# Turning more activations by transposing transfers, issued from ScalarE's queue, in a two-layer encoder trunk

## The chip, the cores and the metric

The kernel runs on one core of a Trainium2 chip. The metric is the device time of one execution in microseconds; the median of several executions is compared. TensorE does the matrix products and the transpositions by identity, ScalarE (ACT) and VectorE (DVE) the elementwise work, GpSimd (POOL) a little, and SyncE (SP) issues most transfers.

## The reference

256 tokens of width 1024 pass two layers. Each layer has one wide projection, two parallel branches, a merge, a feed-forward part and an embedding term. All is float32.

```python
u = rms_norm(h, g_mix_pre)
(gq, gk, gv, gg, ra_f, ra_b, aq, ak, av, gate_a, gate_b) = jnp.split(u @ w_in, offsets, axis=-1)
# branch A: gated linear attention in both directions, 4 heads
o_gla = rms_norm(o_f + o_b, g_gla_out).reshape(b, s, GLA_VAL)
branch_a = (o_gla * jax.nn.silu(gg)) @ w_o_gla
# branch B: grouped-query attention, 8 query heads in 2 groups, axial rotary positions
q = apply_axial_rope(rms_norm(aq.reshape(b, s, ATTN_HEADS, HEAD_DIM), g_q_norm), cos, sin)
branch_b = gqa_attention(q, k, v) @ w_o_attn
mixed = jax.nn.sigmoid(gate_a) * branch_a + jax.nn.sigmoid(gate_b) * branch_b
h = h + rms_norm(mixed @ w_out, g_mix_post)
gate, up = jnp.split(rms_norm(h, g_ffn_pre) @ w_ffn_in, 2, axis=-1)
h = h + rms_norm((jax.nn.silu(gate) * up) @ w_ffn_out, g_ffn_post)
h = h + rms_norm(jax.nn.sigmoid(h @ w_ple_gate) * (p_i @ w_ple_proj), g_ple_post)
```

## The kernel before, in words

Every float32 operand x of a product is split into a high part (x rounded to the type fp32r) and a low part (x minus the high part), and a product is three passes: high by high, high by low, low by high. `split` (L134) makes both parts: ScalarE casts, VectorE subtracts. A weight unit is 1 MB: SP loads it into one of two raw buffers, ScalarE and VectorE split it into one of four pairs of buffers wh and wl (two pieces each), and TensorE uses it in 24 matmuls (`amode` and `passes`, L122, for both halves of 128 tokens). `Stream` keeps the order of the units: `done` frees a pair, starts the next load and places the next splits. Some gates and feed-forward blocks are computed in seven products instead of eight (`seven`, 12 matmuls each); VectorE makes the sums of weights for these (L326 to L337), in tiles called "lent" and "big".

An activation that is the left operand of a product must lie with its channels on the partitions, so it has to be turned. `transpose_in` (L449) does that on TensorE for a block of four 128x128 tiles: four transpositions by the identity into a PSUM bank "aux", then `split` from PSUM. This serves the normalised inputs, the gated output of branch A (tiles "gg" turned into a `Split` object gT), the mix (mixT), the attention's queries (L1267, four heads a group and half) and others.

In the feed-forward part the hidden activations are turned by transfers already, save those of the last pair of blocks. `turn_out` copies the block on ScalarE so that the upper and lower 16-bit words stand apart (L463 or L468), and a transposing transfer of 2-byte elements (L469), issued by SP, turns them. Some ticks later `take_in` joins the words by another copy on ScalarE (L476) and splits the result from SBUF.

The order of the work is fixed when the program is built. Each engine runs its instructions in the order that a planner gives it, mostly that of the program; `high_priority` puts a group of instructions ahead by that many places. Small tasks are generators: `tick` is called after every six matmuls of width 512, and a task yields the number of ticks after which it wants to go on. `need` runs a task to its end at once, for the user of a result. In the gate stage the order is the string GATES: u is a unit of the first branch's gate, a digit one of the seven products of the second's, m a unit of branch A's output projection, which needs gT. Then come the merge (attention's output projection) and "wout", the product of the mix with w_out, first for the first half of the tokens and then for the second.

Of the kernel before, what the change touches and what calls it, by code (L numbers as in the profile page):

```python
# [27 lines left out]
WAIT, WAIT_FIRST = 6, 4  # L28

WAIT_NEXT, WAIT_IN, WAIT_H = (7, 9), ((6, 9), (6, 6)), ((3, 5), (3, 5))  # L30
WAIT_MIX = 3, 6
WAIT_SPREAD = 12
W = dict(r=5, z=6, s0=4, s=3, s1=9, o0=1, o=1, k=4, q=3, a0=1, a1=4, a2=4, a3=1, g=6)

STEPS_FIRST = "00 10 01 11 02 12 03 13".split()
STEPS = "00 01 02 10 03 11 12 13".split()
# [24 lines left out]
def trunk_kernel(ctx: ExitStack, tc: tile.TileContext, a: dict, out: bass.AP):  # L61
# [390 lines left out]
        if plain is not None:  # L452
            nc.scalar.copy(plain, ps[:, : n * P])

    def turn_out(src, k, hf):

        with tc.high_priority(AHEAD):
            both, turned = halves(mid())
            turned = turned.bitcast(U16)
            parts = both.bitcast(U16).rearrange("p (s c) -> p s c", s=2)  # L460
            words = src.bitcast(U16)
            if hf is None:
                nc.scalar.copy(  # L463
                    parts.rearrange("p s (k h f) -> p s k h f", k=2, f=P),
                    words.rearrange("p (h k f s) -> p s k h f", h=2, f=P, s=2),
                )
            else:
                nc.scalar.copy(parts, words.rearrange("p (c s) -> p s c", s=2))  # L468
            nc.sync.dma_start_transpose(out=turned.rearrange("p (x t) -> p x t", t=P), in_=parts.rearrange("p s c -> p (s c)"))  # L469
        return both, turned  # L470

    def take_in(sp, both, turned, k, hf):

        n, tn = (2, T) if hf is None else (4, P)
        hi, lo = sp.at(k, n, (hf or 0) * P, tn)
        nc.scalar.copy(  # L476
            both.bitcast(U16).rearrange("p (k t s) -> p k t s", s=2, t=tn),
            turned.rearrange("p (s k t) -> p k t s", s=2, t=tn),
        )
        split(hi, lo, both.rearrange("p (k t) -> p k t", t=tn))  # L480

    last_pow = [None]

# [565 lines left out]
    for l in range(DEPTH):  # L1049
# [210 lines left out]
        def attend(g):  # L1260
            qs = []
            for hf in range(2):
                yield W["q"]
                ps = aux()
                for i in range(4):
                    hd = 4 * g + i
                    nc.tensor.transpose(ps[:, i * P : (i + 1) * P], qrs[hf][:, hd * P : (hd + 1) * P], ident)  # L1267
                qh, ql = halves(mid(F32R))
                split(qh, ql, ps)
# [193 lines left out]

        ogate = Task(out_gate(), f"{l}gg")

# [49 lines left out]
        def merge(br):  # L1515
            def then(j, hf, o):
                sl = [s[:, hf, j * 512 : (j + 1) * 512] for s in sgate[: br + 1]]
                vmul(sl[br], o, sl[br])
                if br == 1:
                    nc.vector.tensor_tensor(out=sl[0], in0=sl[0], in1=sl[1], op=ALU.add)  # L1520
# [46 lines left out]


        part[0] = f"{l}ffnin"
        hid = Split()  # L1570
        us = [[ws.take() for _ in range(2)] for _ in range(2)]

        def turned(src, k, hf):

            def turn():
                if k == 2 * PAIRS[-1]:
                    yield WAIT_LAST[hf]
                    transpose_in(hid, src, k, 4, hf)
                else:
                    x = turn_out(src, k, hf)  # L1580
                    yield WAIT_TURNED
                    take_in(hid, *x, k, hf)
# [193 lines left out]
```

## Time and profile before

| | us |
|---|---|
| median of 3 runs | 908.38 (907.43 to 909.86) |
| the profiled execution | 909.68 |
| its span | 907.9 |
| TensorE busy | 898.8 |
| VectorE busy | 790.2 |
| ScalarE busy | 620.5 |
| GpSimd busy | 105.9 |

Engines in the rows are PE (matmul), PEld (weight load, beside PE), DVE, ACT, POOL and SP; a q behind the name is the engine's queue of instructions. L134 is line 134 of the kernel. Instructions that issue transfers are not counted as busy. A row of the groups gives the line, the engine, the operation, the tile written and the tiles read, shapes and count, then busy time and mean ns, then idle time just before with what ended it. In a timeline a row begins with its start and its length. The 0 or 1 in a tile's name is the layer, and the letters behind it the part of the program.

### The profile page before, as it was taken

The page shows a single profiled execution, that of the slowest core. Times are in us where ns is not written, and L with a number is a line of the kernel's source. Part 1 is how long each engine was busy: PE and PEld are TensorE (multiplying, and loading weights), DVE is VectorE, ACT ScalarE, POOL GpSimd, SP SyncE. Part 2 cuts the span into 40 slices and gives each one's busy share as a digit, 9 for nine tenths or more (in the row PEclk, how much of TensorE's full clock was granted, in tenths as well). Part 3 has the DMA queues.
Part 4 walks back from the last instruction along what each step waited for, and adds up shares of the span by engine and source line. Part 5 has one row for each costly group of instructions (what it writes and reads, how often), then busy time and mean ns, then how long its engine had stood idle before and what let it go on. Part 6 is the DMA issues. An engine that isn't in the chain of part 4 may idle for free.

```text
span 907.9 us, 12157 instructions
## 1 busy us (share of the span) xinstructions
PE 898.8 (99%) x4479; PEld 762.2 (84%) x4479; DVE 790.2 (87%) x1021; ACT 620.5 (68%) x1011; POOL 105.9 (12%) x157
## 2 busy tenths in 40 slices
PE   9999999999999999999999999999999999999997
PEld 8898888888888887887898888888888888888886
DVE  7999989987668999998779899799876799999984
ACT  7688677564467787756676687675644796958563
POOL 3700221300100000000254001110000000000001
PEclk9999999999999999999999999999999999999999
DMA  8663445657397594956576424455573966858461
GB/s 283 219 189 136 140 140 191 216 187 249 115 288 204 173 301 146 317 170 233 180 279 204 168 93 140 139 186 185 186 241 100 309 180 206 254 210 264 150 231 47
DMA packets 108519, 178.16 MB, mean 196 GB/s; under 512 B 22494, under 2 KB 46566, under 8 KB 107948
## 3 DMA queue, kind: packets, MB, share of 16 engines
q1 hardware_dynamic: 108300, 177.25, 59.9%
q8 instruction: 35, 0.57, 0.3%
q14 instruction: 24, 0.20, 0.1%
q10 hardware_dynamic: 160, 0.14, 0.0%
HBM read 169.50 MB, written 3.15 MB: 190 GB/s over the span
## 4 chain that ended last, share of the span: by engine, by line
PE 78%; DVE 11%; DMA 4%; issue 4%; ACT 2%; POOL 0%; SPq 0%; POOLq 0%; ACTq 0%; DVEq 0%
PE acc_1ffnin L122 12%; PE acc_0gate L122 7%; PE acc_1gate L122 7%; PE acc_1ffnin L106 7%; DVE wl_0ffnin L134 6%; PE acc_1rq L122 3%; PE acc_0gqk L106 2%; PE acc_1gqk L106 2%; PE acc_1wout L122 2%; PE acc_0ple L122 2%; PE acc_1v L122 2%; PE acc_0gg L122 2%; PE acc_1gg L122 2%; PE acc_0v L122 2%; PE acc_0merge L122 2%
## 5 line engine op out<-in xcount | busy, mean ns | idle before, releaser
L134 ACT CAST wh_0ffnin<-raw_0ffnin 128x1024 fp32r<-128x1024 f32 x38 | 38.1, 1048 | 19.8 <-DMA raw_0ffnin<-in_w_ffn_out_dram 10.2
L134 ACT CAST wh_1ffnin<-raw_1ffnin 128x1024 fp32r<-128x1024 f32 x38 | 38.3, 1048 | 17.4 <-DMA raw_1ffnin<-in_w_ffn_out_dram 5.0
L134 DVE TENSOR_TENSOR wl_0ffnin<-raw_0ffnin,wh_0ffnin 128x1024 fp32r<-128x1024 f32 x38 | 44.6, 1219 | 5.8 <-ACT wh_0ffnin L134 5.8
L134 DVE TENSOR_TENSOR wl_1ffnin<-raw_1ffnin,wh_1ffnin 128x1024 fp32r<-128x1024 f32 x38 | 44.8, 1219 | 5.0 <-ACT wh_1ffnin L134 4.9
L106 PE MATMUL acc_0ffnin<-wh_0ffnin,big_0ffnin 128*128 128x512 f32 x176 | 45.4, 392 | 0.0
L106 PE MATMUL acc_1ffnin<-wh_1ffnin,big_1ffnin 128*128 128x512 f32 x176 | 45.1, 390 | 0.0
L122 PE MATMUL acc_0ffnin<-wh_0ffnin,big_0wout 128*128 128x512 f32 x168 | 41.8, 390 | 0.0
L122 PE MATMUL acc_1ffnin<-wh_1ffnin,big_1wout 128*128 128x512 f32 x168 | 41.5, 389 | 0.0
L106 PEld LDWEIGHTS acc_0ffnin<-wh_0ffnin,big_0ffnin 128*128 128x128 f32 x176 | 32.8, 188 | 7.5 <-DVE big_0ffnin L134 0.5
L106 PEld LDWEIGHTS acc_1ffnin<-wh_1ffnin,big_1ffnin 128*128 128x128 f32 x176 | 33.0, 188 | 6.9
L122 PEld LDWEIGHTS acc_0ffnin<-wh_0ffnin,big_0wout 128*128 128x128 f32 x168 | 31.4, 188 | 7.1 <-ACT wh_0ffnin L134 0.4
L122 PEld LDWEIGHTS acc_1ffnin<-wh_1ffnin,big_1wout 128*128 128x128 f32 x168 | 31.5, 188 | 6.5
L134 DVE TENSOR_TENSOR wl_1ffnin<-lent_1ffnin,wh_1ffnin 128x1024 fp32r<-128x1024 f32 x30 | 35.7, 1217 | 0.6 <-ACT wh_1ffnin L134 0.6
L134 DVE TENSOR_TENSOR wl_0ffnin<-lent_0ffnin,wh_0ffnin 128x1024 fp32r<-128x1024 f32 x30 | 35.6, 1216 | 0.1
L134 ACT CAST wh_1ffnin<-lent_1ffnin 128x1024 fp32r<-128x1024 f32 x30 | 30.7, 1051 | 5.4 <-PE acc_1ffnin L106 3.9
L134 ACT CAST wh_0ffnin<-lent_0ffnin 128x1024 fp32r<-128x1024 f32 x30 | 30.4, 1053 | 3.6 <-DVE lent_0ffnin L332 3.4
L134 ACT CAST wh_0gate<-raw_0gate 128x1024 fp32r<-128x1024 f32 x20 | 19.9, 1049 | 14.4 <-DMA raw_0gate<-in_w_o_attn_dram 6.1
L134 ACT CAST wh_1gate<-raw_1gate 128x1024 fp32r<-128x1024 f32 x20 | 19.9, 1048 | 13.9 <-PE acc_1gate L122 5.9
L134 DVE TENSOR_TENSOR wl_0gate<-raw_0gate,wh_0gate 128x1024 fp32r<-128x1024 f32 x20 | 24.2, 1257 | 5.2 <-ACT wh_0gate L134 5.1
L134 DVE TENSOR_TENSOR wl_1gate<-raw_1gate,wh_1gate 128x1024 fp32r<-128x1024 f32 x20 | 23.5, 1221 | 5.1 <-ACT wh_1gate L134 5.1
L106 PE MATMUL acc_0ffnin<-wl_0ffnin,big_0ffnin 128*128 128x512 f32 x88 | 24.6, 394 | 0.6 <-DVE wl_0ffnin L134 0.6
L106 PE MATMUL acc_1ffnin<-wl_1ffnin,big_1ffnin 128*128 128x512 f32 x88 | 24.0, 391 | 0.0
(730 smaller groups left out, 2731.7 us busy)
## 6 DMA issues: line engine op xcount, KB each, us to landing
raw_0ffnin<-in_w_ffn_out_dram SPq DMA_DIRECT2D x11, 1024.0 KB, 5.9
raw_1ffnin<-in_w_ffn_out_dram SPq DMA_DIRECT2D x11, 1024.0 KB, 5.5
lent_0ffnin<-in_w_ffn_in_dram SPq DMA_DIRECT2D x6, 1024.0 KB
lent_1ffnin<-in_w_ffn_in_dram SPq DMA_DIRECT2D x6, 1024.0 KB, 7.5
raw_0v<-in_w_in_dram SPq DMA_DIRECT2D x4, 1024.0 KB, 5.8
raw_0gate<-in_w_o_gla_dram SPq DMA_DIRECT2D x4, 1024.0 KB, 6.8
raw_0gate<-in_w_o_attn_dram SPq DMA_DIRECT2D x4, 1024.0 KB, 5.2
raw_0wout<-in_w_ffn_in_dram SPq DMA_DIRECT2D x8, 512.0 KB, 4.6
```

What stands on the lines that cost most here:

```text
L106: return nc.tensor.matmul(o, lhsT, rhs, start=start, stop=stop)
L122: nc.tensor.matmul(o, x, y, start=start and n == 0, stop=stop and n == len(seq) - 1, **kw)
L134: return nc.scalar.copy(hi, src), nc.vector.tensor_tensor(out=lo, in0=src, in1=hi.bitcast(F32), op=ALU.subtract)
```

## The change

Three more kinds of activations are turned by transfers, in both layers:

- the gated outputs of branch A: all four blocks of a layer (two halves of tokens, two halves of channels);
- the mix: three of four blocks; the second half of the channels for the first half of the tokens stays on TensorE;
- the queries of the second head group: both halves; they are sent out after the softmax of the first group and joined where the transposition was.

All transposing transfers, those of the feed-forward part too, are issued from ScalarE's queue. A transfer writes into the tile it came from, and the scratch for the parted words is a tile whose content is used up: the pre-gate values for the gated outputs, the second gate for the mix, the first group's queries for the second's. The feed-forward part takes half a tile of scratch instead of a whole one. The numbers of ticks are new: 9 and 11 (then 1 more for each second block) instead of 6 for the gated outputs, and 5, 7 and 3, 8 instead of 3, 6 for the mix.

```diff
-WAIT_MIX = 3, 6
+WAIT_MIX = (5, 7), (3, 8)
-W = dict(r=5, ..., a3=1, g=6)
+W = dict(r=5, ..., a3=1)
+WAIT_GATED = 9, 11
...
-    def turn_out(src, k, hf):
+    def turn_out(src, parts, mixed=False):
         with tc.high_priority(AHEAD):
-            both, turned = halves(mid())
...
+            planes, words = (t.bitcast(U16) for t in (parts, src))
+            if mixed:
                 nc.scalar.copy(
-                    parts.rearrange("p s (k h f) -> p s k h f", k=2, f=P),
+                    planes.rearrange("p (s k h f) -> p s k h f", s=2, k=2, f=P),
                     words.rearrange("p (h k f s) -> p s k h f", h=2, f=P, s=2),
                 )
             else:
-                nc.scalar.copy(parts, words.rearrange("p (c s) -> p s c", s=2))
-            nc.sync.dma_start_transpose(out=turned.rearrange("p (x t) -> p x t", t=P), in_=parts.rearrange("p s c -> p (s c)"))
-        return both, turned
+                nc.scalar.copy(planes.rearrange("p (s c) -> p s c", s=2), words.rearrange("p (c s) -> p s c", s=2))
+            nc.scalar.dma_start_transpose(out=words.rearrange("p (x t) -> p x t", t=P), in_=planes)
+
+    def take_in(hi, lo, src, parts):
+        tn = hi.shape[-1]
         nc.scalar.copy(
-            both.bitcast(U16).rearrange("p (k t s) -> p k t s", s=2, t=tn),
-            turned.rearrange("p (s k t) -> p k t s", s=2, t=tn),
+            parts.bitcast(U16).rearrange("p (k t s) -> p k t s", s=2, t=tn),
+            src.bitcast(U16).rearrange("p (s k t) -> p k t s", s=2, t=tn),
         )
-        split(hi, lo, both.rearrange("p (k t) -> p k t", t=tn))
+        split(hi, lo, parts.rearrange("p (k t) -> p k t", t=tn))
...
+                if g == 0:
+                    ps = aux()
+                    for i in range(4):
+                        nc.tensor.transpose(ps[:, i * P : (i + 1) * P], qrs[hf][:, i * P : (i + 1) * P], ident)
+                    split(qh, ql, ps)
+                else:
+                    take_in(*(t.rearrange("p (i t) -> p i t", t=P) for t in (qh, ql)), *halves(qrs[hf])[::-1])
...
                 prs.append(softmax(g, hf, qs[hf]))
+                if g == 0:
+                    turn_out(*halves(qrs[hf])[::-1])
...
-                turn_in(gT, sg, hf, W["g"])
+                xs = [(t, gg[:, hf, j * 512 : (j + 1) * 512]) for j, t in enumerate(halves(sg))]
+                for x in xs:
+                    turn_out(*x)
+
+                def turn(hf=hf, xs=xs):
+                    for j, x in enumerate(xs):
+                        yield WAIT_GATED[hf] if j == 0 else 1
+                        take_in(*gT.at(4 * j, 4, hf * P, P), *x)
...
                     def turn():
-                        yield WAIT_MIX[hf]
-                        transpose_in(mixT, sl[0], 4 * j, 4, hf)
+                        if (j, hf) != (1, 0):
+                            turn_out(*sl)
+                        yield WAIT_MIX[j][hf]
+                        if (j, hf) != (1, 0):
+                            take_in(*mixT.at(4 * j, 4, hf * P, P), *sl)
+                        else:
+                            transpose_in(mixT, sl[0], 4 * j, 4, hf)
...
-                    x = turn_out(src, k, hf)
+                    if not spare:
+                        spare.extend(halves(mid()))
+                    parts = spare.pop()
+                    turn_out(src, parts, hf is None)
                     yield WAIT_TURNED
```

More of the change, by code (lines that the diff above doesn't have):

```diff
@@ L453, in transpose_in @@
             nc.scalar.copy(plain, ps[:, : n * P])
-    def turn_out(src, k, hf):
+    def turn_out(src, parts, mixed=False):
         with tc.high_priority(AHEAD):
-            both, turned = halves(mid())
[L459 to L462, printed above, removed]
+            planes, words = (t.bitcast(U16) for t in (parts, src))
+            if mixed:
                 nc.scalar.copy(
-                    parts.rearrange("p s (k h f) -> p s k h f", k=2, f=P),
+                    planes.rearrange("p (s k h f) -> p s k h f", s=2, k=2, f=P),
                     words.rearrange("p (h k f s) -> p s k h f", h=2, f=P, s=2),
@@ L1263, in attend @@
                 yield W["q"]
[L1264 to L1267, printed above, removed]
                 qh, ql = halves(mid(F32R))
-                split(qh, ql, ps)
+                if g == 0:
[5 more added lines that the diff above has]
+                    take_in(*(t.rearrange("p (i t) -> p i t", t=P) for t in (qh, ql)), *halves(qrs[hf])[::-1])
                 qs.append((qh, ql, qss[hf][:, 4 * g : 4 * g + 4]))
@@ L1461, in out_gate @@
                     vmul(t, t, on[:, hf, s])
-                turn_in(gT, sg, hf, W["g"])
+                xs = [(t, gg[:, hf, j * 512 : (j + 1) * 512]) for j, t in enumerate(halves(sg))]
[5 more added lines that the diff above has]
+                        take_in(*gT.at(4 * j, 4, hf * P, P), *x)
+                gT.makers[hf].append(Task(turn(), part[0]))
         ogate = Task(out_gate(), f"{l}gg")
@@ L1569, in trunk_kernel @@
         part[0] = f"{l}ffnin"
-        hid = Split()
+        hid, spare = Split(), []
         us = [[ws.take() for _ in range(2)] for _ in range(2)]
@@ L1579, in turn @@
                 else:
-                    x = turn_out(src, k, hf)
+                    if not spare:
+                        spare.extend(halves(mid()))
+                    parts = spare.pop()
+                    turn_out(src, parts, hf is None)
                     yield WAIT_TURNED
-                    take_in(hid, *x, k, hf)
+                    take_in(*(hid.at(k, 2, 0, T) if hf is None else hid.at(k, 4, hf * P, P)), src, parts)
             t = Task(turn(), part[0], k // 4)
```

5 lines of the change are left out of this document (1 added, 4 removed).

## The prediction

> **What bounds the kernel now.** I read the page first: the busy times, the slices and the chain that ended last.
>
> ```profile
> span 907.9 us, 12157 instructions
> PE 898.8 (99%) x4479; PEld 762.2 (84%) x4479; DVE 790.2 (87%) x1021; ACT 620.5 (68%) x1011; POOL 105.9 (12%) x157
> DVE  7999989987668999998779899799876799999984
> ACT  7688677564467787756676687675644796958563
> PEclk9999999999999999999999999999999999999999
> ```
>
> TensorE is busy for 898.8 of 907.9 us at its full granted clock. Then the waits of TensorE:
>
> ```profile
> PE acc_0ffnin L106 <- DVE wl_0ffnin L134: 0.6, 2, 0.3
> PE acc_0ffnin L122 <- DVE wl_0ffnin L134: 0.2, 1, 0.2
> ```
>
> Inside the layers it hardly waits; what it waits for is the low part of a weight from VectorE. So an instruction taken from TensorE is worth its full time as long as the weights keep coming. They come in a fixed order: load, high part on ScalarE, low part on VectorE, matmul. The third view is therefore the stages, with each engine's room. The columns are length, PE, PEld, DVE, ACT and POOL busy, clock, DMA share, GB/s.
>
> ```profile
> 57.00:75.00 18.00, 18.00 (x109) 15.92 (x108) 17.11 (x36) 17.31 (x37) 0.00 (x0) 1.00 0.67 222
> 75.00:101.00 26.00, 26.00 (x144) 22.37 (x143) 26.00 (x42) 19.83 (x42) 5.61 (x4) 1.00 0.26 88
> 143.40:167.60 24.20, 24.20 (x116) 20.27 (x115) 24.20 (x27) 17.36 (x22) 0.00 (x0) 1.00 0.39 126
> 167.60:191.00 23.40, 23.40 (x105) 19.38 (x104) 23.28 (x21) 11.82 (x15) 10.47 (x10) 1.00 0.69 238
> 203.00:228.00 25.00, 25.00 (x116) 20.65 (x115) 19.08 (x22) 11.96 (x14) 0.00 (x0) 1.00 0.73 246
> 760.00:800.00 40.00, 40.00 (x178) 33.13 (x177) 38.31 (x39) 34.87 (x42) 0.00 (x0) 1.00 0.80 237
> ```
>
> VectorE has no room at all while the gated outputs are turned (24.20 of 24.20) and in the value stage (26.00 of 26.00). ScalarE has 6.8 us there and 6.2 us in the value stage. TensorE is the bound, VectorE stands right behind it, and ScalarE feeds VectorE.
>
> **The change: what TensorE is spared.** The prices of a transposition:
>
> ```profile
> L1267 PE MATMUL aux_0at<-ident,mid_0rq x16: 270/272/274, 45.6 to 97.5; 128*128 128x128 f32 x16
> 147.86 1.75 PE aux_0gg L449 x16
> 201.31 14.96 PE acc_0merge L122 x66
> 216.71 4.13 PE acc_0merge L122 x18
> ```
>
> The sixteen of the gated outputs hold the chain for 1.75 us. Four of the mix hold it for 216.71 - (201.31 + 14.96) = 0.44 us. The queries' have the same shape and latency, so 0.44 us for four. Spared per layer are 16 of the gated outputs (1.75), 12 of the mix (3 x 0.44 = 1.32) and 8 of the second query group (2 x 0.44 = 0.88): 3.95 us, in two layers 7.9 us. The PSUM banks that they used come free too, which I cost at nothing since TensorE waits for none.
>
> **What ScalarE gets.** The feed-forward part does it already, so each step has a row:
>
> ```profile
> L468 ACT COPY mid_0ffnin<-t_0ffnin x6: 1038/1044/1047, 267.2 to 376.0; 128x1024 uint16<-128x1024 uint16 x6
> L469 SPq DMA_TRANSPOSE mid_0ffnin<-mid_0ffnin x9: 1237/1250/1922, 268.3 to 377.1; - x9
> DMA to landing us min/median/max: 3.3/3.6/4.3
> L476 ACT COPY mid_0ffnin<-mid_0ffnin x9: 1168/1177/1183, 274.0 to 380.8; 128x1024 uint16<-128x1024 uint16 x9
> L134 ACT CAST big_0ffnin<-mid_0ffnin 128x512 fp32r<-128x512 f32 x9 | 5.5, 622 | 0.1
> L134 DVE TENSOR_TENSOR big_0ffnin<-mid_0ffnin,big_0ffnin 128x512 fp32r<-128x512 f32 x9 | 6.1, 684 | 0.5 <-ACT big_0ffnin L134 0.5
> L134 DVE TENSOR_TENSOR big_0gg<-aux_0gg,big_0gg 128x512 fp32r<-128x512 f32 x4 | 2.5, 678 | 0.0
> ```
>
> A block of four tiles costs ScalarE a copy that parts the words (1.04), the issue (1.24; the queue is another engine's in the row, and I take the same time on ScalarE's), and the copy that joins them (1.18): 3.46 us. High part and low part cost what they cost from PSUM (0.68 on VectorE in both rows), so VectorE is neither helped nor loaded. There are 9 such blocks a layer, 18 in all: 62 us. The feed-forward part's 18 transfers also move from SyncE's queue to ScalarE: 18 x 1.24 = 22 us. Together 85 us on an engine that has 287 idle. Only its places matter.
>
> SyncE loses those 18 issues and their waits for ScalarE; the weight loads behind them can start earlier. The transfers no longer stand behind weight loads in one queue, and ScalarE's wait for them may shrink:
>
> ```profile
> SPq L469 <- ACT wh_0ffnin L134: 14.7, 4, 6.4
> ACT mid_0ffnin L476 <- DMA mid_0ffnin<-mid_0ffnin: 12.0, 5, 5.8
> ACT mid_1ffnin L476 <- DMA mid_1ffnin<-mid_1ffnin: 3.2, 3, 1.7
> ```
>
> In the feed-forward parts I set 22 us of issues against these 15.2 us and take zero: even in the fullest stretch, 760 to 800, four issues bring ScalarE from 34.87 to 39.8 of 40. If the cover fails, it costs about 1 us a layer. POOL's queue is not touched. The source tile now stays in use until its join, while each transfer takes half a tile less of scratch. I cost that at nothing, the tile being one of five; where they ran out, the next gate's SiLU would wait for a join, 1.18 us.
>
> **Gated outputs, where it is tight.** Added between 143.4 and 167.6 are four blocks, 13.8 us, where ScalarE has 24.20 - 17.36 = 6.8. It comes out 7.0 us late. What it feeds, at the third of the seven products of the branch gate and at the third unit of the first merge:
>
> ```profile
> 162.41 1.06 ACT L134 CAST wh_0gate<-lent_0gate 128x1024 fp32r<-128x1024 f32 x1 [1.17 <-PE acc_0gate L122]
> 165.60 3.49 DVE L134 TENSOR_TENSOR wl_0gate<-lent_0gate,wh_0gate 128x1024 fp32r<-128x1024 f32 x3
> 173.04 1.07 PE L122 MATMUL acc_0gate<-wl_0gate,mid_0gate 128*128 128x512 f32 x4
> 181.79 2.57 DVE L134 TENSOR_TENSOR wl_0gate<-raw_0gate,wh_0gate 128x1024 fp32r<-128x1024 f32 x2
> 186.64 1.07 PE L122 MATMUL acc_0gate<-wl_0gate,big_0gg 128*128 128x512 f32 x4
> ```
>
> VectorE starts on the cast 2.1 us after it ends (165.60 - 163.47); of the 7.0 us it would lose up to 4.9. It cannot catch up before 191, and at the third merge unit its lead on TensorE is 186.64 - 184.36 = 2.3 us, of which 1.75 go because TensorE comes earlier. So the upper end is 4.9 - 0.5 = 4.4 us of stall a layer. The lower end is 0: two of the four join copies (2.4 us) belong to the second half of the channels and can run behind the casts, and if half of the issues (2.5) run beside a cast already sent to the engine, ScalarE is 2.1 us late, no more than VectorE's distance. Below nothing I see no way, since the spared time is counted already. I take 1.0 us a layer, near the lower end, because two of the three needed reliefs are a matter of order alone.
>
> **Queries.** Two copies with issues (4.6 us) fall between 57 and 75, where ScalarE has 0.7 us, and the late two joins (2.4) in the next stage. After 75 ScalarE has 6.2 us, which takes them up; VectorE, full there, may lose some. Lower end 0, upper end 4.6 - 0.7 = 3.9 if all of it reached TensorE. The casts that follow are for weights used a unit later, so I take 0.25 a layer.
>
> **Mix.** ScalarE has 25.00 - 11.96 = 13.0 us for 10.4. The tightest block is the first half's first:
>
> ```profile
> 211.99 2.00 ACT L134 CAST wh_0merge<-raw_0gate 128x1024 fp32r<-128x1024 f32 x2 [2.00 <-DMA raw_0gate<-in_w_out_dram]
> 212.06 0.69 DVE L1520 TENSOR_TENSOR big_0gate<-big_0gate,big_0gate 128x512 f32<-128x512 f32 x1
> 216.62 2.00 ACT L134 CAST wh_0merge<-raw_0gate 128x1024 fp32r<-128x1024 f32 x2 [2.63 <-DMA raw_0gate<-in_w_out_dram]
> 223.87 0.39 PE L122 MATMUL acc_0wout<-wh_0merge,big_0merge 128*128 128x512 f32 x1
> ```
>
> Ready at 212.75, parted by 215.0 (behind the two casts), landed by 218.6, joined by 219.8, split by 221.1. TensorE wants it at 223.87 - 0.88 = 223.0, so 1.9 us are left. The join waits for the landing, with the casts of the output projection queued behind it; they have the same 1.9. Ends 0 and 1 us (a landing of 4.3 with one cast ahead), I take 0.25 a layer. The longer waits (9 and 11 ticks for the gated outputs, a tick being six matmuls) only place the joins later and cost TensorE nothing themselves.
>
> **Sum.** -7.9 + 2 x (1.0 + 0.25 + 0.25) = -4.9 us. The profiled execution took 909.68 us (span 907.9 and 1.8 around it); it would take 904.8. It lies 1.3 above the median of the runs, 908.38, so the median becomes **903.5 us**. Its own range is 901.5 to 905.6.
>
> [...]
>
> **The rivals.** (1) Clean: orders and copies fit everywhere, all stalls 0. For it: 287 idle us of ScalarE. 908.4 - 7.9 = 900.5.
>
> (2) VectorE takes TensorE's place: it is full from 143 to 191 and from 75 to 101, so what TensorE is spared there turns into waits for low parts. Against it: 2.3 us of lead at the third merge unit, more than 1.75. If the gated and query shares are lost (2 x (1.75 + 0.88) = 5.3), -2.6 remain: 905.8, and with the stalls I took about 907.
>
> (3) Slower: ScalarE falls behind as the feeder in the gate stage, at the upper ends, 4.4 there and 1 in each feed-forward part, with nothing of the issue beside other work: -7.9 + 2 x (4.4 + 1 + 0.5) = +3.9, so 912.3. Losses of 3.95 us a layer cancel the gain; it is slower beyond the noise from 5.3. For it: 13.8 us into 6.8. Against it: two joins are not due until later.
>
> (4) The transfers land late beside the weight loads. One in the chain took 5.66 us:
>
> ```profile
> 268.26 5.66 DMA mid_0ffnin<-mid_0ffnin
> ```
>
> With that the mix block comes 2.1 us later, just past its 1.9: +0.4 in all, still faster. It makes the kernel slower only from about 11 us. At 12 us it gives 2 x (12 - 3.6 - 1.9) - 7.9 = +5.1, 913.5.
>
> **How the numbers follow.** Forecast 0.42, clean 0.16, VectorE 0.20, ScalarE 0.19, late landing 0.03. About 0.3%, 2.7 us, is what a measurement of this kernel can tell from no change. Faster 0.58, same 0.20, slower 0.22. The range takes in the clean case and VectorE's and reaches to ScalarE's: 900 to 912.5.
>
> **What would show it.** TensorE's busy time 7.9 us lower; ScalarE's about 40 higher (issues are not counted), with gaps of about 1.2 us behind each parting copy. In the stretch from 143 to 191, waits of the gate's matmuls for low parts of 1 us a layer, and idle time of VectorE behind ScalarE's casts. The forecast is wrong if those waits pass 4 us a layer, if TensorE waits for a joined block at the output projection, or if the transfers land later than 5 us.

## The result, and the profile after

The changed kernel took 967.39 us (median of 5 runs, 965.45 to 971.0), the kernel before 908.38: a ratio of 1.065 (95% interval 1.062 to 1.069), 59.0 us slower. The forecast was 903.5 us, in a range of 900 to 912.5. The profiled execution took 971.0 us with a span of 969.3.

From the page of the changed kernel, the busy times, the slices, the transfer queues (packets, MB, share of 16 engines; q1 holds SP's transfers, q10 the transposing ones) and the chain that ended last:

```profile
span 969.3 us, 12052 instructions
PE 919.3 (95%) x4407; PEld 763.8 (79%) x4407; DVE 792.5 (82%) x1021; ACT 656.5 (68%) x1047; POOL 103.5 (11%) x157
PEclk9989999999999898999999999999999999999999
q1 hardware_dynamic: 89292, 172.53, 52.0%
q10 hardware_dynamic: 38176, 9.58, 6.5%
PE 43%; DVE 18%; DMA 17%; ACT 14%; issue 6%; ACTq 1%; POOL 1%; SPq 0%; POOLq 0%; DVEq 0%
```

The 72 transpositions are gone from TensorE (4479 matmuls before, 4407 now), and yet it is busy 20 us longer and idle 50 us instead of 9. Busy time rose because the granted clock fell in places: the trace's record of it shows one half in eight stretches of 3.4 or 6.8 us, 37.5 us in all, where the kernel before shows none until its last 3.9 us. Half of that, some 19 us, is an estimate of what the clock took of the 59. The last section comes back to it. In the chain TensorE's share fell to 43%, and transfers have 17%. What ScalarE and TensorE wait for in the changed kernel (us in total, times, longest):

```profile
ACT mid_0ffnin L472 <- DMA t_0ffnin<-mid_0ffnin: 34.1, 6, 10.7
ACT mid_1ffnin L472 <- DMA t_1ffnin<-mid_1ffnin: 23.7, 5, 9.4
...
PE acc_0ffnin L123 <- ACT wh_0ffnin L135: 11.8, 5, 4.3
PE acc_1ffnin L123 <- ACT wh_1ffnin L135: 6.5, 2, 3.6
```

The waits of ScalarE for turned blocks in the feed-forward parts, 12.0 and 3.2 us before, are 34.1 and 23.7 now, and TensorE waits there for high parts of weights from ScalarE, which no wait of the kernel before named. By stages, first of the kernel before and then of the changed one (columns as in the prediction):

```profile
260.00:340.00 80.00, 79.64 (x352) 64.64 (x351) 69.02 (x73) 60.38 (x77) 0.00 (x0) 1.00 0.79 234
340.00:456.00 116.00, 115.17 (x544) 95.05 (x543) 105.67 (x108) 79.79 (x105) 9.69 (x9) 1.00 0.63 210
```

```profile
260.00:340.00 80.00, 72.31 (x305) 58.83 (x305) 58.46 (x65) 51.89 (x74) 2.28 (x5) 0.94 0.62 198
340.00:456.00 116.00, 109.42 (x460) 85.39 (x459) 98.35 (x92) 75.64 (x88) 0.95 (x1) 0.97 0.66 200
```

Between 260 and 456 us TensorE started 896 matmuls before and 765 now, with less of everything else done too. So the largest loss is in the feed-forward part, which the change touches, but for its scratch tiles, only in who issues its transfers. The chain shows the first of them (start, length, what), and a timeline the loads that SP issued beside it:

```profile
279.85 10.70 DMA t_0ffnin<-mid_0ffnin
```

```profile
279.70 1.27 SPq L298 DMA_DIRECT2D lent_0ffnin<-in_w_ffn_in_dram  x2
```

The transfer was issued 0.15 us behind the first of two loads of 1 MB and 0.76 us ahead of the second, and its block was joined 10.70 us later. In the kernel before, the same two loads stood behind the same transfer in SyncE's queue, and it took 5.66 us:

```profile
268.26 1.92 SPq L469 DMA_TRANSPOSE mid_0ffnin<-mid_0ffnin  x1
270.23 1.25 SPq L297 DMA_DIRECT2D lent_0ffnin<-in_w_ffn_in_dram  x2
```

All 36 transfers of the changed kernel take, from issue to landing:

```profile
DMA to landing us min/median/max: 3.1/4.9/8.3
```

Before it was 3.3/3.6/4.3. (The view stays below the 10.70 that ScalarE waited in the chain; by the packet records the last piece of that transfer was through 10.1 us after its issue.)

### The profile page after: what moved, and what is told of

Read it like the earlier page. It is cut to its first block, busy times and chain, and to the rows that moved or that the text cites. A ratio compares the mean times of both kernels' runs of the same rounds, so it can differ in the third digit from the quotient of the medians.

```text
span 969.3 us, 12052 instructions
## 1 busy us (share of the span) xinstructions
PE 919.3 (95%) x4407; PEld 763.8 (79%) x4407; DVE 792.5 (82%) x1021; ACT 656.5 (68%) x1047; POOL 103.5 (11%) x157
## 3 DMA queue, kind: packets, MB, share of 16 engines
q1 hardware_dynamic: 89292, 172.53, 52.0%
q10 hardware_dynamic: 38176, 9.58, 6.5%
## 4 chain that ended last, share of the span: by engine, by line
PE 43%; DVE 18%; DMA 17%; ACT 14%; issue 6%; ACTq 1%; POOL 1%; SPq 0%; POOLq 0%; DVEq 0%
DMA t_0ffnin<-mid_0ffnin 5%; PE acc_1ffnin L123 4%; DMA t_1ffnin<-mid_1ffnin 3%; PE acc_1ffnin L107 3%; DVE wl_1gate L135 3%; DVE wl_0ffnin L135 3%; ACT wh_0ffnin L135 3%; PE acc_0ffnin L107 3%; PE acc_1rq L123 2%; PE acc_0ple L123 2%; PE acc_0gate L123 2%; PE acc_1v L123 2%; PE acc_1ple L123 2%; PE acc_0wout L123 2%; PE acc_0ffnin L123 2%
## 5 line engine op out<-in xcount | busy, mean ns | idle before, releaser
L123 PE MATMUL acc_0ffnin<-wh_0ffnin,big_0wout 128*128 128x512 f32 x168 | 44.9, 412 | 8.2 <-ACT wh_0ffnin L135 8.2
L107 PE MATMUL acc_1ffnin<-wh_1ffnin,big_1ffnin 128*128 128x512 f32 x176 | 47.2, 399 | 4.8 <-ACT wh_1ffnin L135 4.7
L123 PEld LDWEIGHTS acc_1ffnin<-wh_1ffnin,big_1wout 128*128 128x128 f32 x168 | 32.2, 192 | 10.1 <-ACT wh_1ffnin L135 3.3
L472 ACT COPY mid_0ffnin<-t_0ffnin 128x1024 uint16<-128x1024 uint16 x9 | 10.5, 1165 | 34.9 <-DMA t_0ffnin<-mid_0ffnin 34.1
L107 PE MATMUL acc_1ffnin<-wl_1ffnin,big_1ffnin 128*128 128x512 f32 x88 | 26.4, 412 | 2.8 <-DVE wl_1ffnin L135 2.8
L123 PE MATMUL acc_1ffnin<-wh_1ffnin,mid_1ffnin 128*128 128x512 f32 x96 | 25.2, 407 | 3.6 <-ACT wh_1ffnin L135 3.6
L123 PE MATMUL acc_0ffnin<-wh_0ffnin,mid_0ffnin 128*128 128x512 f32 x96 | 24.5, 398 | 3.5 <-ACT wh_0ffnin L135 3.5
```

The costliest lines, as they stand in the source:

```text
L107: return nc.tensor.matmul(o, lhsT, rhs, start=start, stop=stop)
L123: nc.tensor.matmul(o, x, y, start=start and n == 0, stop=stop and n == len(seq) - 1, **kw)
L472: nc.scalar.copy(parts.bitcast(U16).rearrange("p (k t s) -> p k t s", s=2, t=tn), src.bitcast(U16).rearrange("p (s k t) -> p k t s", s=2, ...
```

## The experiments

Differences are to the kernel before on the same chip: 909.5 us for the first three, 910.0 for the next four, 910.2 for the four after those, 911.5 for the last two.

**SyncE issues all transfers.** One word of the changed kernel:

```diff
-            nc.scalar.dma_start_transpose(out=words.rearrange("p (x t) -> p x t", t=P), in_=planes)
+            nc.sync.dma_start_transpose(out=words.rearrange("p (x t) -> p x t", t=P), in_=planes)
```

> The changed kernel with one word back: SyncE issues all transposing transfers, so they stand in one queue with the weight loads again. Theory Q (a queue of their own makes the transfers share the DMA engines with the weight loads piece by piece, so they land late): landings return to 3.3 to 4.3 us, ScalarE's wait for them in the feed-forward parts falls from 57.8 us to about 15, and the time is 899 to 908 us, because the 7.9 us of transpositions are then really spared. Theory S (ScalarE's added work, 62 us of copies and issues and 22 us of moved issues, starves VectorE): only the 45 us of issues leave ScalarE, the 40 us of copies stay, and the time is 915 to 940 us.

It took 918.5 us, 9.0 above the kernel before (ratio 1.0096, 1.0064 to 1.0127). Of the 59 us, 50 lie in the queue that the transfers are issued from. The waits of the feed-forward parts are back at 13.0 us, as theory Q said, but the time is not in its range; it lies in that of theory S, 915 to 940. What TensorE still waits for:

```profile
PE acc_1wout L123 <- ACT big_1merge L135: 3.2, 2, 2.3
PE acc_0wout L123 <- ACT big_0merge L135: 2.9, 2, 2.4
PE aux_1at L107 <- ACT big_1kv L135: 2.2, 1, 2.2
PE aux_0merge L450 <- DVE big_0gate L1529: 1.2, 1, 1.2
PE aux_0at L107 <- ACT big_0kv L135: 1.1, 1, 1.1
```

Parts of the mix come late at the output projection, and the keys come late at the scores. Not every late part of the mix is one that a transfer turned: the longest wait of each layer (2.4 and 2.3 us) ends with the cast of the block that is still turned on TensorE, which stands on ScalarE behind the parting copy of the last block. No wait of the gate stage is left, although all four gated blocks are turned by transfers there.

**The kernel before, with ScalarE issuing.** The same word, in the kernel before:

```diff
-            nc.sync.dma_start_transpose(out=turned.rearrange("p (x t) -> p x t", t=P), in_=parts.rearrange("p s c -> p (s c)"))
+            nc.scalar.dma_start_transpose(out=turned.rearrange("p (x t) -> p x t", t=P), in_=parts.rearrange("p s c -> p (s c)"))
```

> The kernel before with one word changed: ScalarE issues the 18 transposing transfers of the feed-forward parts, nothing else is new. Theory Q: ScalarE's wait for them rises from 15.2 us to 40 or more, landings of 5 to 13 us, and the time is 940 to 960 us, most of the loss of the whole change. Theory S: ScalarE gets 22 us of issues where it has 27 us of room a layer, and the time is 908 to 915 us.

It took 954.6 us, 45.0 above the kernel before (1.0495, 1.0457 to 1.0533). Nothing was added or removed but the place of 18 issues; ScalarE's waits for the turned blocks are those of the changed kernel:

```profile
ACT mid_0ffnin L476 <- DMA mid_0ffnin<-mid_0ffnin: 33.5, 5, 11.0
ACT mid_1ffnin L476 <- DMA mid_1ffnin<-mid_1ffnin: 22.8, 7, 8.3
```

**Is it ScalarE's time?** With SyncE issuing, each parting copy was done twice, which gives ScalarE 36 x 1.04 us more to do:

```diff
                 nc.scalar.copy(planes.rearrange("p (s c) -> p s c", s=2), words.rearrange("p (c s) -> p s c", s=2))
+                nc.scalar.copy(planes.rearrange("p (s c) -> p s c", s=2), words.rearrange("p (c s) -> p s c", s=2))
```

(the same for the form with `mixed`).

> As the run with SyncE issuing everything, but each parting copy is done twice on ScalarE (36 copies more, 1.04 us each, 37 us), which stands for the time that the issues took there. Theory Q: within 4 us of that run. Theory S: most of the loss comes back, 940 us or more.

It took 925.5 us, 6.9 more than with single copies (918.5): more than the 4 us of theory Q, far from the 940 of theory S. 37 us of added work cost 6.9; the 36 issues, 45 us by their 1.25, cost 50. The engine's time alone doesn't account for it.

**The landing by itself.** A small kernel turns a block of 128 x 1024 elements of 2 bytes in six settings, three times each:

```diff
+    phase("_alone", False, 512, 0, 0)
+    phase("_ownb", False, 512, 4, 0)
+    phase("_owna", False, 128, 4, 0)
+    phase("_ownc", False, 1024, 4, 0)
+    phase("_samea", True, 512, 1, 3)
+    phase("_sameb", True, 512, 2, 2)
```

The arguments are: issued by SyncE or not, the loads' row in elements of 4 bytes, and how many loads of 1 MB SyncE issues ahead of the transfer and behind it.

> No trunk at all, x is copied to the output: one transposing transfer of a 128x1024 two-byte tile, three times in each of six settings. Alone; from ScalarE's queue beside four 1 MB loads from SyncE's queue with rows of 2 KB, of 512 bytes and of 4 KB; and from SyncE's own queue behind one load or two, with the others behind it. Theory Q: alone 3 to 4 us; beside the loads on another queue 8 us or more with 2 KB rows, later still with 4 KB rows and sooner with 512-byte rows; in the same queue 4 to 8 us from the issue, the wait for the loads ahead included, and little more than alone once its turn has come. Theory S: 3 to 5 us in all six.

Its transfers, with the median us to landing, and the timeline of one setting:

```profile
turned_alone<-parts_alone ACTq DMA_TRANSPOSE x3, 3.1
turned_ownb<-parts_ownb ACTq DMA_TRANSPOSE x3, 12.2
turned_owna<-parts_owna ACTq DMA_TRANSPOSE x3, 7.4
turned_ownc<-parts_ownc ACTq DMA_TRANSPOSE x3, 13.2
turned_samea<-parts_samea SPq DMA_TRANSPOSE x3, 5.7
turned_sameb<-parts_sameb SPq DMA_TRANSPOSE x3, 8.1
```

```profile
24.14 1.61 ACTq L79 DMA_TRANSPOSE turned_ownb<-parts_ownb  x1
36.14 1.16 ACT L79 COPY joined_ownb<-turned_ownb 128x1024 uint16<-128x1024 uint16 x1 [12.02 <-DMA turned_ownb<-parts_ownb]
38.01 0.20 ACT L79 COPY raw<-tiny 128x4 f32<-128x4 f32 x1 [0.72 <-DMA raw<-in_w_ffn_out_dram]
```

A transfer alone lands in 3.1 us. From a queue of its own beside four loads with rows of 2 KB it takes 12.2, and is joined at 36.1, 1.9 us before the last of the loads is through at 38.0. In SyncE's queue it lands 5.7 us after its issue behind one load and 8.1 behind two: it waits for the loads ahead of it, while those behind it (three and two) cost it nothing that shows. With rows of 512 bytes beside it in the other queue it takes 7.4, with 4 KB 13.2. The packet records of this trace show the two queues sharing by pieces: with rows of 2 KB, 1123 to 1244 pieces of the loads pass while the 1056 of the transfer do (12,672 over 12 transfers), about one for one. The transfer has the small pieces: in the changed kernel, 38,176 packets for 9.58 MB on q10 are 251 bytes each, 89,292 for 172.53 MB on q1 are 1932. The order of the settings fits with that: 7.4, 12.2 and 13.2 us as the rows beside the transfer grow. The rest of the 12.2 us is a late start. Alone the first piece moves 1.2 us after the issue begins, beside the loads 4.1 to 5.2 us after it; what holds it back isn't shown.

Two of the four loads beside the transfer were issued just ahead of it and two just behind, as in the last setting with one queue. So 12.2 against 8.1 us compares the same four loads: from another queue the two issued behind the transfer run beside it. It doesn't show that a second queue is slower in itself: behind all four loads in SyncE's queue a transfer would take about 13 us, an estimate from 2.4 to 2.6 us for each load ahead, which no run tried.

**Which of the new blocks cost.** With SyncE issuing, first the gated outputs alone (the mix and the queries as in the kernel before):

```diff
-                        if (j, hf) != (1, 0):
-                            turn_out(*sl)
-                        yield WAIT_MIX[j][hf]
...
+                        yield WAIT_MIX[hf]
+                        transpose_in(mixT, sl[0], 4 * j, 4, hf)
...
-                if g == 0:
-                    turn_out(*halves(qrs[hf])[::-1])
```

> Only the gated outputs are turned by transfers; the mix and the second query group stay on TensorE, and SyncE issues all transfers. Theory L (each block is lost where its consumer already waits: the mix at the output projection, the queries at the keys; the gated outputs are covered): TensorE is spared 2 x 1.75 = 3.5 us and nothing new waits, so 3.5 below the kernel before, 905 to 906. Rival V (each of the 18 blocks costs ScalarE and VectorE the same wherever it lies; with SyncE issuing all of them the time rose by 9.0 although 7.9 were spared, so 16.9 / 18 = 0.94 us a block): 8 blocks cost 7.5 against 3.5 spared, 4 above the kernel before, about 913.

Then the gated outputs with the queries, and the gated outputs with the mix; each takes back only one of the two edits above:

> Gated outputs and queries by transfers, SyncE issuing; the mix on TensorE. Theory L: 5.3 us spared; the waits of the first score matmuls for the keys' ScalarE copies, 1.1 and 2.2 us with all blocks turned, remain, and the stretch from 57 to 75 us keeps its lower clock (9% of 18 us, up to 1.6): 0.5 to 2 us below the kernel before, 907 to 908.5. Rival V: 12 blocks cost 11.3 against 5.3 spared, 6 above, about 915.

> Gated outputs and 12 of the mix's blocks by transfers, SyncE issuing; the queries on TensorE. Theory L: 6.1 us spared; the stalls at the output projection remain (4.0 and 3.0 us without work on TensorE in the two stretches, and the waits of the merge before, about 2, and what the clock loses behind them): 3 to 7 us above the kernel before, 912 to 916. Rival V: 14 blocks cost 13.1 against 6.1 spared, 7 above, about 916. This run tells the two apart only together with the two others: by L the gated outputs alone and this differ by 7 to 10, by V by 3.

| turned by transfers, SyncE issuing | us | to the kernel before | ratio (95%) |
|---|---|---|---|
| gated outputs | 906.9 | -3.1 | 0.9959 (0.9945 to 0.9973) |
| gated, queries | 909.0 | -1.0 | 0.9992 (0.9980 to 1.0003) |
| gated, mix | 912.9 | +2.9 | 1.0031 (1.0021 to 1.0041) |
| all three | 918.5 | +9.0 | 1.0096 (1.0064 to 1.0127) |

V falls, and the three runs lie close to theory L: one in its range, two above it, by 0.9 us (905 to 906) and 0.5 us (907 to 908.5). The gated outputs give 3.1 of the 3.5 us that TensorE is spared, the queries cost 2.1 net and the mix 6.0. Together that makes +5.0; with all three it is 9.0, and of the 4.0 between them only 1.7 are explained (the clock, below).

**Only the feed-forward part's transfers back on SyncE**, the 18 new ones on ScalarE:

```diff
+            queue.dma_start_transpose(out=words.rearrange("p (x t) -> p x t", t=P), in_=planes)
...
+                    turn_out(src, parts, hf is None, nc.sync)
```

> The changed kernel, with the feed-forward part's 18 transfers issued by SyncE again and the 18 new ones by ScalarE. Theory Q (a transfer lands late when it has a queue of its own beside large weight loads): the feed-forward part loses its waits of 34 and 24 us, and the new blocks keep landings of 4 to 6 us; the time is that of all transfers on SyncE, 918.5, plus up to 2 us of later landing for the mix: 918 to 925. Rival S (what costs is any issue on ScalarE): half of the issues stay, and of the 49 us between the changed kernel and the one with SyncE issuing about half, 940 or more.

It took 926.6 us, 16.5 above the kernel before (1.0175, 1.0156 to 1.0194). So 42.5 of the 59.0 us are the feed-forward part's queue, close to the 45.0 of that edit alone. Rival S (940 or more) falls. The rest is 7.5 above the run with SyncE issuing everything, and theory Q's range (918 to 925) is missed by 1.6. The next run finds most of that.

**The gated outputs alone, issued by ScalarE:**

> Only the gated outputs by transfers, these issued by ScalarE, the feed-forward part's by SyncE. It measures by itself the stall of the gate stage that the prediction put at 1.0 us a layer (0 to 4.4). With all new blocks issued by ScalarE TensorE stood 2.2 us a layer still between 140 and 191 us; with SyncE issuing the same blocks 0 to 0.2. If these 2.2 come from the gate's own transfers: 908.4 to 910, level with the kernel before to 0.4% above the run with SyncE issuing. If they come from the queries or the mix, or from their clock: 906.9 as with SyncE.

It took 914.4 us, 4.2 above the kernel before (1.0044, 1.0030 to 1.0059) and 7.3 above SyncE issuing the same, about as much as that rest and above both expectations. Between the two profiled executions it is 4.7 us, and TensorE's waits for the gate's weights are 4.9 us longer. No wait of ScalarE for these transfers is in its trace. ScalarE's timeline at the start of the gate stage, first of this run and then with SyncE issuing:

```profile
144.58 1.99 ACT L466 COPY big_0gg<-mid_0gg 128x1024 uint16<-128x1024 uint16 x2 [1.50 <-DVE mid_0gg L128]
145.66 3.47 ACTq L467 DMA_TRANSPOSE mid_0gg<-big_0gg  x2
149.17 1.99 ACT L466 COPY big_0gg<-mid_0gg 128x1024 uint16<-128x1024 uint16 x2 [2.59 <-DVE mid_0gate L135]
150.24 2.64 ACTq L467 DMA_TRANSPOSE mid_0gg<-big_0gg  x2
152.98 2.00 ACT L135 CAST wh_0gate<-lent_0gate 128x1024 fp32r<-128x1024 f32 x2 [1.82 <-PE acc_0gate L123]
```

```profile
144.72 2.00 ACT L466 COPY big_0gg<-mid_0gg 128x1024 uint16<-128x1024 uint16 x2 [1.50 <-DVE mid_0gg L128]
146.62 1.05 ACT L135 CAST wh_0gate<-lent_0gate 128x1024 fp32r<-128x1024 f32 x1
147.57 1.99 ACT L466 COPY big_0gg<-mid_0gg 128x1024 uint16<-128x1024 uint16 x2
```

Four issues take 6.1 us of ScalarE's own sequence (3.47 + 2.64). Behind them stands the first cast of the gate's weights, which begins at 152.98 instead of 146.62. The first issue of a pair begins beside a copy already sent to the engine (145.66, with the second copy running to 146.57), but what stands behind it waits until the issues are through.

**The mix: is it the place of its transfers in SyncE's queue?** Gated outputs, and of the mix only the last block:

```diff
+                        if (j, hf) == (1, 1):
+                            turn_out(*sl)
+                        yield WAIT_MIX[j][hf]
+                        if (j, hf) == (1, 1):
+                            take_in(*mixT.at(4 * j, 4, hf * P, P), *sl)
+                        else:
+                            transpose_in(mixT, sl[0], 4 * j, 4, hf)
```

> Gated outputs by transfers as in the run that has them alone, and of the mix only the last block (second half, second four tiles), SyncE issuing. With 12 of the mix's blocks the first w_out load landed at 229.1 in place of 227.1 or earlier: SyncE issued a transfer on either side of it. Theory M1 (the mix loses because the first two transfers stand between the output projection's weight loads in SyncE's queue; the last one comes behind them): 2 x 0.44 us more spared than with the gated outputs alone and no new wait: 905.5 to 906.5 beside 906.9 for the gated outputs alone. Rival M2 (each block of the mix is late for its own consumer, 6.0 + 2.6 us over six blocks): 2 x 1.4 - 0.9 = 2 us above the gated outputs alone, 909.

It took 910.5 us (1.0003, 0.9988 to 1.0017), 3.4 above the gated outputs alone: M1 is refuted for this block, which has the weight loads behind it, and M2 (909) named less than was measured. TensorE's waits at the output projection, 1.4 us in this layer and 1.7 in the other, are not for this block. ScalarE's timeline, with the cast of the third block in time, which TensorE turned:

```profile
229.66 1.04 ACT L466 COPY big_0gate<-big_0gate 128x1024 uint16<-128x1024 uint16 x1 [1.01 <-DVE big_0gate L1525]
230.61 0.58 ACT L135 CAST big_0merge<-aux_0merge 128x512 fp32r<-128x512 f32 x1
```

TensorE had turned the third block by 228.0. ScalarE was free at 228.6, stood for 1.01 us until the last block came from VectorE, parted it, and only then cast the third; TensorE's wait of 1.42 us ends with that cast, at 231.24. The last block itself is joined at 233.9 and has its high part at 235.7, 6.1 us after it was finished, and TensorE runs on without a gap for 10 us. With all of the mix's blocks on transfers (SyncE issuing) the waits of 2.4 and 2.3 us end in the same way, and only 0.45 and 0.84 us with a block that a transfer turned. So most of what the mix waits is the place of a parting copy in ScalarE's order, and `high_priority` moves these copies ahead. The mix without it was not run, and whether its first two blocks lose by their place between the loads was not tried alone.

**The queries without being moved ahead:**

```diff
-                    turn_out(*halves(qrs[hf])[::-1])
+                    turn_out(*halves(qrs[hf])[::-1], ahead=0)
```

> Gated outputs and queries by transfers, SyncE issuing, but the copies that part the queries' words stand in ScalarE's order where the text has them, not moved ahead. Theory K (two copies of 0.95 to 1.04 us were put ahead of the casts of the keys, and TensorE waited 1.1 to 1.5 us a layer for those): the waits for the keys' ScalarE copies fall under 0.3 us, and 1.5 to 3 us come back: 905 to 907.5 beside 909.0. Rival R (what costs is ScalarE's room between 48 and 75 us, wherever the copies lie): 909 to 911, with the wait at another tile.

It took 907.7 us (0.9972, 0.9959 to 0.9985), 1.5 us less against its kernel before than with the copies moved ahead. The waits for the keys' ScalarE copies are gone; one of 1.6 us came in their place (`aux_0at` for VectorE's `mid_0at`). Theory K holds for about half. In this order the two copies of layer 0 stand at 47.0 and 55.4 us; moved ahead, the second stood at 51.4, just before the keys' casts. This version and the one with the gated outputs alone beat both kernels; their intervals overlap.

**Does ScalarE lose by standing in the join's wait?** The kernel before with ScalarE issuing, and the joins later by ticks:

```diff
-WAIT_TURNED, WAIT_LAST = 9, (3, 4)
+WAIT_TURNED, WAIT_LAST = 14, (3, 4)
```

> The kernel before with ScalarE issuing the feed-forward part's transfers (954.6), and the joins 14 ticks behind their transfers in place of 9; a tick is six matmuls of 0.39 us, so they come 5 x 2.3 = 11.7 us later. Theory W (what TensorE loses is that ScalarE stands in the join's wait, up to 9.4 to 10.7 us at a time, with the casts of the weights queued behind it): the transfers, 4 to 12 us long, have landed before the join comes up, ScalarE's waits of 33.5 and 22.8 us fall below 10 each, and the time comes to 910 to 925. Rival D (the block itself comes too late for the second product of the feed-forward part): later joins bring nothing or make it worse, 954 or more, with TensorE waiting for joined blocks.

It took 952.4 us, 42.2 above the kernel before, with waits for transfers of 39.0 and 14.9. That looks like rival D, but ScalarE's timeline shows that the first join didn't move: the planner still put it directly behind its transfer.

```profile
269.89 1.33 ACTq L469 DMA_TRANSPOSE mid_0ffnin<-mid_0ffnin  x1
280.67 1.16 ACT L476 COPY mid_0ffnin<-mid_0ffnin 128x1024 uint16<-128x1024 uint16 x1 [10.81 <-DMA mid_0ffnin<-mid_0ffnin]
```

The run tells nothing apart. (Five ticks are also less than was expected: 66 matmuls take 14.96 us in the prediction's row, so six take 1.4 us and five ticks 6.8, not 11.7.) So the joins were tied to a place, each behind the cast that the text has last before it:

```diff
-        return nc.scalar.copy(hi, src), nc.vector.tensor_tensor(out=lo, in0=src, in1=hi.bitcast(F32), op=ALU.subtract)
+        casts[0] = nc.scalar.copy(hi, src); return casts[0], nc.vector.tensor_tensor(out=lo, in0=src, in1=hi.bitcast(F32), op=ALU.subtract)
...
-        nc.scalar.copy(
+        with tc.issue_after(split.__defaults__[0][0].ins): nc.scalar.copy(
```

> The kernel before with ScalarE issuing the feed-forward part's transfers (954.6), and each join's copy tied behind the cast written last before it in the text, so that 2 to 9 casts and copies stand between a transfer and its join in ScalarE's order, where the first join stood directly behind its transfer. Theory W (TensorE loses because ScalarE stands in the join's wait, with the weight casts behind it): ScalarE's waits for transfers, 33.5 and 22.8 us, fall to 15 or less in all, and the time to 912 to 928. Rival D (the turned block itself comes too late, 7 to 12 us after its issue in place of 3.6): TensorE waits for the joined block in place of the weights, and the time stays above 945.

It took 933.2 us, 21.7 above the kernel before (1.0248, 1.0216 to 1.0281). ScalarE's waits for transfers fell from 56 to 16 us, and 23 of the 45 us came back. D (above 945) falls, and W named up to 928, 5 us less than measured. A row of its chain and two of ScalarE's timeline say what holds the rest in layer 0:

```profile
379.21 16.04 DMA mid_0ffnin<-mid_0ffnin
```

```profile
383.14 4.71 ACTq L469 DMA_TRANSPOSE mid_0ffnin<-mid_0ffnin  x1
387.89 2.00 ACT L134 CAST wh_0ffnin<-big_0ffnin 128x1024 fp32r<-128x1024 f32 x2 [3.83 <-issue]
```

One transfer took 16 us, and the issue of the next one, 4 us behind it, took 4.71 instead of 1.25, with a weight cast behind it. So even where the join stands later, slower transfers and issues (16.04 and 4.71 us here) still reach TensorE.

The same tie for every join of the changed kernel:

> The changed kernel (967.4) with every join tied behind the cast written last before it, in the feed-forward part, for the gated outputs, the mix and the queries. Theory W: of the 41 us that the feed-forward part's issue costs here (967.4 less 926.6 with SyncE issuing those) most come back, 930 to 945; the rest, of the gate stage, the mix and the keys, stays, since there ScalarE's own issues and the blocks' own lateness cost it. Rival D: above 955.

It took 957.3 us (1.0535, 1.0487 to 1.0582), 45.8 above the kernel before instead of 59.0. 13 us came back, fewer than the 22 to 37 that W named, and the time lies where rival D was set (above 955). ScalarE's waits for the feed-forward part's blocks did fall, from 57.8 to 12.4 us. In this run TensorE waits 4.8 and 4.9 us for the mix at the output projection, longer than with any other order, so the tie also moved joins that had no time to spare. How the remaining loss divides between late landing, long issues and late joins stays open.

## Why the prediction was wrong

**Feed-forward part: this step failed, with 42.5 us.** The prediction set 22 us of issues against 15.2 us of waits that "may shrink", because the transfers "no longer stand behind weight loads in one queue", and took zero, with 1 us a layer if the cover failed; measured are 21 a layer. The landing of 3.3 to 4.3 us was read as a property of the transfer. It was one of its place: in SyncE's queue a transfer waited for the loads ahead of it (5.7 us to landing behind one, 8.1 behind two) and ran ahead of the next ones. From a queue of its own it shared with all loads under way: 12.2 in the small kernel against 8.1 in one queue with the same loads and 3.1 alone. With the joins tied to later places 23 of the 45 us came back in the kernel before, so there about half of the loss is ScalarE standing in the join's wait; how the rest divides between late landing and long issues stays open. Rival 4 named that mechanism and had a point from which it decides, 11 us. It was given 0.03, and was counted for the mix alone, where the forecast had a margin; the 18 transfers of the feed-forward part, where ScalarE stands in the wait with the weights' casts behind it, weren't put into it. Its 12 us is the small kernel's landing (in the changed kernel ScalarE waited up to 10.7); its 913.5 us missed the place.

**TensorE's spared time: right in size where it stands alone.** The gated outputs alone give 3.1 us of the 3.5 worked out. For the mix and the queries it was not measured by itself.

**Gate stage: the taken value failed, the bounds held.** Taken were 1.0 us a layer between 0 and 4.4. With ScalarE issuing it is (3.5 + 4.2) / 2 = 3.9, with SyncE (3.5 - 3.1) / 2 = 0.2. The mechanism is rival 3's, ScalarE falling behind as the feeder. The relief that failed is "if half of the issues (2.5) run beside a cast already sent to the engine": they began beside copies, and the casts stood behind them.

**Queries: wrong place.** Two copies with issues were placed between 57 and 75 us. Even in the order of the text they stand at 47.0 and 55.4, and `high_priority` brings the second to 51.4, ahead of the keys' casts. The description of the kernel names that mechanism; the prediction didn't apply it. Taken were 0.25 us a layer, measured (2.1 + 1.8) / 2 = 1.9 with SyncE issuing, within the ends of 0 and 3.9; in the order of the text it is (0.6 + 1.8) / 2 = 1.2.

**Mix: mis-sized.** Taken were 0.25 us a layer, at most 1; measured (6.0 + 2.6) / 2 = 4.3. The prediction worked out the first block as the tightest, with an end of 1 us that its own terms don't give (0.7 us of landing and 1.0 for a cast are within the 1.9 that are left). The last block, which it didn't work out, alone costs (3.4 + 0.9) / 2 = 2.2, and not by its own latency: its parting copy holds up the cast of another block on ScalarE. It is the mechanism of the queries again, and the prediction has no term for it. The sign that the prediction named, TensorE waiting for a joined block at the output projection, is there with SyncE issuing, but small (0.45 and 0.84 us).

**VectorE as the bound** (rival 2) didn't come to it: VectorE is busy for 82% and waits for ScalarE, and the gated outputs, whose share that rival gave up, alone bring 3.1 of their 3.5 us.

## What to carry to other kernels

A landing time read from a trace belongs to the queue and to what stands in it and beside it (3.1 us alone, 8.1 behind two loads in one queue, 12.2 beside four from another): before a transfer is moved to another queue, look for the loads that would then run beside it, and at what the engine has queued behind the wait. An issue is work of the engine that issues, 1.25 us at the median here, and 4.71 where one came 4 us behind a transfer that took 16; give it to the engine whose queue nobody needs next. Of several moves of one kind take each alone: of three here one was a gain (0.4%), one lost 0.6 to 2.1 us by its order, and one lost 6.0. And a copy that is moved ahead holds up what stands behind it on its engine: here the casts of the keys (TensorE waited 1.08 us for them, layer 0, gated outputs and queries) and of a block of the mix (1.42 us, its last block alone).

## What was not expected of the hardware

A stall of TensorE cost more than its length in one run. In two runs TensorE waited alike for the keys, 1.13 and 0.38 us in one (all three kinds of blocks on transfers, SyncE issuing) and 1.08 and 0.38 in the other (gated outputs and queries). Behind it the same ten score matmuls took 2.34 us in the first and 1.36 in the second:

```profile
55.50 0.38 PE L107 MATMUL aux_0at<-big_0kv,mid_0at 128*128 128x256 f32 x1 [1.13 <-ACT big_0kv L135]
57.60 2.34 PE L107 MATMUL aux_0at<-big_0kv,mid_0at 128*128 128x256 f32 x10
```

```profile
55.37 0.38 PE L107 MATMUL aux_0at<-big_0kv,mid_0at 128*128 128x256 f32 x1 [1.08 <-ACT big_0kv L135]
57.29 1.36 PE L107 MATMUL aux_0at<-big_0kv,mid_0at 128*128 128x256 f32 x10
```

The granted clock from 56 to 60 us was 0.65 in the first run and 1.00 in the second. From 56 to 64 us the clock cost the first run some 1.7 us (4 x 0.35 + 4 x 0.08). In the records of the granted clock, in all traces of the whole kernel, the clock changes on a grid of 3.41 us; a window is here one step of that grid. In the first run all of the wait, 1.72 us, fell into one window (53.81 to 57.22), and the next was at half the clock; in the second it lay across an edge (55.49), 1.08 us on one side and 0.59 on the other. Half the clock also followed windows that were idle only in part: of 3886 windows at full clock (without the first 20 us and the last 8 of each trace), 35 were followed by one at half: none with less than 1.69 us of idle time (neither matmul nor weight load), and every one with more than 1.84 us. So of these two stalls of about half a window, the one that fell into a single window cost 1.7 us more. The other surprise is the landing of a transfer beside loads (12.2 us against 3.1 alone), told with the small kernel above.
